# Hybrid decoder trunk on one core: the clearing of the forget gate's tile is moved to the head of GpSimd's row of constants

## The chip, the cores and the metric

The kernel runs on one core of one Trainium2 chip. The metric is the device time of one execution in microseconds. Three executions of the kernel before took 1278.13, 1283.45 and 1277.13 us; their median is 1278.13. A further execution was recorded by the hardware profiler, and all rows below come from that one.

## The reference

Two layers, each with two sub-layers. The first sub-layer is the mixer, which this case is about:

```
u = rms_norm(h, pre_g);  z = u @ w_in
q, k, v, f_logit, a_val, a_gate, sc_b, sc_c, sc_x = split(z)
log_f  = log_sigmoid(f_logit + b_forget)            # 8 heads
y_attn = forgetting_attention(q, k, v, log_f)       # logit[t,s] = q.k/8 + F[t] - F[s], F = cumsum(log_f)
y_conv = silu(layer_norm(conv31(a_val * sigmoid(a_gate)))) @ a_pw_w
y_sc   = sc_b * conv3(sc_c * sc_x)
h     += rms_norm(head_norm([y_attn, y_conv, y_sc]) @ w_out, post_g)
```

The second sub-layer is a gated feed-forward network with a three-tap convolution. The sequence has 512 tokens and 16 learned ones ahead of them, 528 rows in all; the model is 1024 wide.

## The kernel before, in words

Activations lie transposed, features on the 128 partitions and the 528 rows along the free axis, cut into two halves of 264. Each float32 operand is split into a high and a low part (`uhi`, `ulo`; `whi`, `wlo`), and a product takes three TensorE passes (hi*hi, lo*hi, hi*lo). ScalarE casts a landed weight block to its high part (line 608) and VectorE makes the low part (line 612).

The order of the instructions on TensorE, ScalarE, VectorE and GpSimd is written by a planner in the kernel (`Flow`), which carries its own estimates of durations, and it is kept as written: every engine works through its queue strictly in that order. GpSimd's row of constants is not planned. It stands in the source in the order in which it runs.

The mixer of a layer begins with six weight blocks (two for the gate, two for the value of the convolution, then `sc_c` and `sc_x`), whose products are made at line 709. Blocks 1 to 5 lie in the "wide" tiles on the right-hand side of SBUF. When these products have been issued, the pool `ap` is opened over the same memory (line 1025), and its tiles are declared one after the other: `vhi`, `vlo`, `vals`, `causal`, eight `k` tiles, eight `q` tiles, `dm0`, `dm1`, `fx`, `gt`, and smaller ones. GpSimd clears or fills them as they are declared: its row runs from `vhi` (through the helper at line 439) to `causal` (lines 1122 and 1123), four rounds of two pieces of a `k` tile and two of a `q` tile, `dm0` and `dm1`, then `fx` (line 1151), `p4`, `p4w` and last a strip of the tile `both`.

In the compiled program the tiles of `ap` lie in the order in which they are declared, from byte 173,664 of each partition upwards. `fx` has 160 bytes at 228,320. The first `k` tile (`k00`) ends at byte 192,416. The wide tile with the high part of block 5 (`sc_x`) begins at byte 192,480, so `k00` ends 64 bytes short of it. Where a tile of `ap` overlaps a wide tile, its clearing waits for the last product that reads that wide tile: the first `q` tile waits for blocks 2 and 3, the second `k` tile (`k10`) for the last product of block 5. `k00` waits for neither. The layout and these waits are the same in both layers.

Then the projections run on TensorE, in this order near the change: `v` for heads 0 to 3 together with the eight columns of the forget gate, in five blocks of rows b = 0 to 4 (line 1204, and line 1199 for the short block 4, which reads `both`), two halves of `q`, two of `k`, and so on (line 668). The five blocks and the halves after them take PSUM banks 0, 1, 2, 0, 1, 2, ... in turn, so block 3 needs the bank of block 0 back. What empties a block's bank: ScalarE casts the values to `vhi` (line 1180), VectorE adds the bias of the forget gate and writes `fx` (line 1184), then VectorE makes `vlo` (line 1181). Block 4 goes through the copy `vsum` (lines 1218 and 1219).

The forget gate follows: ScalarE's Abs, Exp and Ln (lines 1231 to 1233), VectorE's lines 1234 to 1239 (four running sums into `fpre`, the last of them read by the product at line 1244), the product with a triangle of ones (lines 1243 and 1244), its copy to `gt` (line 1245), and five transposes (line 1253). Between these stand, in VectorE's queue, the taps of the 31-tap convolution (line 937, `cacc`), the taps of the short convolution (lines 987 and 989, `sccx`), low parts of weights and low parts of `q` and `k` (lines 1292 and 1320).

Of the kernel before, what the change touches and what calls it, by code (L numbers as in the profile page):

```python
# [9 lines left out]
F32 = mybir.dt.float32  # L10
# [5 lines left out]
P = 128  # L16
# [6 lines left out]
HEADS = 8  # L23
# [363 lines left out]
def tile_hybrid_trunk(ctx: ExitStack, tc: tile.TileContext, xT, wflat, pv_d, out):  # L387
    nc = tc.nc
# [3 lines left out]
    def T(pool, shape, dt, tag, bufs=None):  # L392
        uid[0] += 1
        kw = {} if bufs is None else {"bufs": bufs}
        return pool.tile(list(shape), dt, tag=tag, name=f"{tag}_{uid[0]}", **kw)
# [498 lines left out]
    def mixer(l, ypool, first, close_first, spans):  # L894
# [130 lines left out]
        ap = ms.enter_context(tc.tile_pool(name=f"ap{l}", bufs=1, side="right", reuse_waits="tile"))  # L1025
# [84 lines left out]
        sc_done = {}  # L1110


        vhi = T(ap, [P, 5, WHOLE, VW], F32R, "vhi")
        vlo = T(ap, [P, 5, WHOLE, VW], F32R, "vlo")
        pw_place[0] = lambda: T(ap, [P, 5, WHOLE, VW], F32R, "vlo").rearrange("p b h d -> p (b h d)")
# [30 lines left out]
        for j in range(2):  # L1146
            dm = T(ap, [P, L], F32R, f"dm{j}")
            mset(dm[:, :N_META], 0.0)
            dms.append(dm)
        fx = T(ap, [P, 5, HEADS], F32, "fx")  # L1150
        nc.gpsimd.memset(fx, 0.0)
        gt = T(ap, [P, 5, HEADS], F32, "gt")
        g_hl = [T(mp, [P, L], F32, "sq", 2)[:HEADS].bitcast(F32R) for _ in range(2)]

# [654 lines left out]
    for l in range(DEPTH):  # L1809
# [15 lines left out]
        with ExitStack() as ms, tc.manual_schedule(engines=every):  # L1825
            flow.yields = YM[l]
            y, y_at, early = mixer(l, ypool, first, wxs.close, i_spans)
# [711 lines left out]
```

## Time and profile before

| | |
|---|---|
| median of three runs | 1278.13 us (1277.13 to 1283.45) |
| the profiled execution | 1277.56 us, of which 1275.8 us span from the first to the last instruction |
| mean granted TensorE clock | 0.995 |
| busy: TensorE, VectorE, ScalarE, GpSimd | 97%, 76%, 61%, 19% of the span |
| TensorE without a product in flight, 50 to 70 us and 70 to 82 us (layer 0) | 0.86 us and 1.38 us |
| the same, 679 to 699 us and 699 to 711 us (layer 1) | 0.65 us and 1.38 us |

A row of a timeline gives the start, the time, the engine, the line, the operation and its tiles; a row that ends in "x2" joins two instructions. What stands in brackets is the idle time of that engine just before, and the instruction that ended it. A row of a list of waits gives who waited for whom, the total in us, how many times, and the longest.

### The profile page before, as it was taken

Reading aid. Unit: us, or ns where it says so; the run is one execution under the profiler, and the core shown is the slowest. Engines: PE = TensorE matmul, PEld = TensorE weight load, DVE = VectorE, ACT = ScalarE, POOL = GpSimd, SP = SyncE. Lnnn points to the kernel's source line nnn. Section 1 sums busy time; section 2 is a strip of 40 time slices with the busy share of each in tenths; the row PEclk is TensorE's granted clock in tenths of the full one; section 3 lists DMA queues with packets and bytes.
Section 4 is the critical chain, followed back from the end, with each engine's and each line's share of the span. In section 5 each row is a group of like instructions: output and inputs, shape, how many; then the busy total and the mean of one; then the engine's idle time right before and its main releaser. Section 6 shows DMA issues by size and latency. Waiting matters only on the chain.

```text
span 1275.8 us, 24511 instructions
## 1 busy us (share of the span) xinstructions
PE 1239.5 (97%) x9468; PEld 1188.3 (93%) x9468; DVE 967.7 (76%) x1752; ACT 775.6 (61%) x1571; POOL 236.2 (19%) x415
## 2 busy tenths in 40 slices
PE   9999999999999999999999999999998999999996
PEld 8988988999999999999999899889997999999986
DVE  7598877588866777788676988766887587778865
ACT  7256668667755555556672666785676565556552
POOL 1314320002122222120003233200022122122200
PEclk9999999999999999999999999999999999999998
DMA  7131131636486866776340322216386677768641
GB/s 225 51 102 52 47 113 34 206 119 167 102 195 139 188 156 154 172 161 183 115 140 18 111 76 68 60 58 213 131 175 136 155 160 169 163 148 185 144 141 66
DMA packets 73942, 165.85 MB, mean 130 GB/s; under 512 B 8081, under 2 KB 26641, under 8 KB 73313
## 3 DMA queue, kind: packets, MB, share of 16 engines
q1 hardware_dynamic: 52048, 124.86, 30.6%
q0 software_dynamic: 21360, 39.02, 19.0%
q8 instruction: 74, 1.21, 0.4%
q10 hardware_dynamic: 416, 0.40, 0.1%
q14 instruction: 44, 0.35, 0.1%
HBM read 129.14 MB, written 8.65 MB: 108 GB/s over the span
## 4 chain that ended last, share of the span: by engine, by line
PE 79%; DVE 8%; ACT 4%; issue 4%; DMA 2%; POOL 2%; DVEq 0%; ACTq 0%; POOLq 0%
PE psum L668 37%; PE psum L2198 25%; PE psum L709 6%; PE psum L1462 2%; PE psum L1204 2%; PE psum L792 2%; PE psum L1405 1%; DVE cacc L937 1%; DMA c<-acc 1%; DMA raw<-in_w_dram 1%; PE psum L1361 1%; POOL q L439 1%; DMA raw<-u 1%; POOL k L439 1%; PE psum L1532 1%
## 5 line engine op out<-in xcount | busy, mean ns | idle before, releaser
L668 PE MATMUL psum<-yhi,whi 128*128 128x264 f32 (+3 forms) x660 | 187.9, 299 | 3.6 <-ACT yp L2373 2.1
L668 PE MATMUL psum<-ylo,whi 128*128 128x264 f32 (+3 forms) x660 | 184.7, 295 | 1.1 <-DVE ylo L2175 0.8
L668 PE MATMUL psum<-yhi,wlo 128*128 128x264 f32 (+3 forms) x660 | 184.3, 294 | 0.2 <-DVE wlo L612 0.2
L668 PE MATMUL psum<-uhi,whi 128*128 128x264 f32 (+1 forms) x640 | 165.2, 291 | 1.2 <-DVE q L1292 1.2
L668 PE MATMUL psum<-ulo,whi 128*128 128x264 f32 (+1 forms) x640 | 161.0, 284 | 0.5 <-DVE ulo L1947 0.5
L668 PE MATMUL psum<-uhi,wlo 128*128 128x264 f32 (+1 forms) x640 | 160.7, 284 | 0.0
L2124 DVE SCALAR_TENSOR_TENSOR c<-z,pv,c 128x528 f32<-128x528 f32 (+1 forms) x156 | 117.1, 757 | 29.0 <-ACT c L2122 26.4
L612 DVE TENSOR_TENSOR wlo<-raw,whi 128x1024 fp32r<-128x1024 f32 (+2 forms) x84 | 100.5, 1205 | 38.1 <-ACT whi L608 37.1
L668 PEld LDWEIGHTS psum<-yhi,whi 128*128 128x128 f32 x660 | 120.3, 188 | 9.1 <-ACT yp L2373 2.5
L668 PEld LDWEIGHTS psum<-ylo,whi 128*128 128x128 f32 x660 | 120.4, 188 | 4.4 <-DVE ylo L1088 1.1
L668 PEld LDWEIGHTS psum<-yhi,wlo 128*128 128x128 f32 x660 | 120.4, 189 | 3.2 <-DVE wlo L612 0.6
L668 PEld LDWEIGHTS psum<-uhi,whi 128*128 128x128 f32 x640 | 111.9, 188 | 4.4 <-issue 2.4
L2211 ACT COPY z<-psum 128x264 f32<-128x264 f32 (+2 forms) x128 | 48.2, 377 | 107.2 <-PE psum L2198 106.5
L668 PEld LDWEIGHTS psum<-ulo,whi 128*128 128x128 f32 x640 | 112.2, 188 | 0.9 <-DVE ulo L1947 0.7
L668 PEld LDWEIGHTS psum<-uhi,wlo 128*128 128x128 f32 x640 | 112.1, 188 | 0.4 <-DVE wlo L612 0.4
L608 ACT CAST whi<-raw 128x1024 fp32r<-128x1024 f32 (+2 forms) x84 | 85.8, 1034 | 38.7 <-DMA raw<-in_w_dram 20.4
L937 DVE SCALAR_TENSOR_TENSOR cacc<-apad,pv,cacc 128x528 f32<-128x528 f32 x120 | 88.6, 766 | 0.3
L709 PE MATMUL psum<-uhi,whi 128*128 128x264 f32 (+1 forms) x320 | 85.0, 289 | 1.3 <-ACT uhi L840 1.3
L709 PE MATMUL psum<-uhi,wlo 128*128 128x264 f32 (+1 forms) x320 | 83.4, 283 | 0.0
L2052 DVE TENSOR_TENSOR wlo<-raw,whi 128x1024 fp32r<-128x1024 f32 (+4 forms) x78 | 76.4, 980 | 8.6 <-ACT whi L2049 8.2
L2049 ACT CAST whi<-raw 128x1024 fp32r<-128x1024 f32 (+4 forms) x78 | 66.3, 855 | 15.5 <-PE psum L668 10.3
L2198 PE MATMUL psum<-uhi,whi 128*128 128x264 f32 (+1 forms) x256 | 72.8, 284 | 2.2 <-ACT yp L2373 2.2
(317 smaller groups left out, 3732.4 us busy)
## 6 DMA issues: line engine op xcount, KB each, us to landing
raw<-in_w_dram SPq DMA_DIRECT2D x110, 512.0 KB
u<-in_w_dram SPq DMA_DIRECT2D x32, 512.0 KB
u<-in_w_dram POOLq DMA_DIRECT2D x32, 256.0 KB, 5.3
raw<-in_w_dram POOLq DMA_DIRECT2D x32, 256.0 KB, 4.1
u<-raw POOLq DMA_DIRECT2D x32, 256.0 KB, 4.0
raw<-u POOLq DMA_DIRECT2D x32, 256.0 KB, 4.2
raw<-in_w_dram SPq DMA_DIRECT2D x16, 448.0 KB
h_mid<-h SPq DMA_DIRECT2D x4, 1056.0 KB
```

The lines of the kernel that those rows point to most:

```text
L439: nc.gpsimd.memset(t.bitcast(F32), val)
L608: nc.scalar.copy(box["hi"][:, :sz], box["raw"][:, :sz])
L612: nc.vector.tensor_sub(lo[:, :sz], box["raw"][:, :sz], box["hi"][:, :sz].bitcast(F32))
L668: nc.tensor.matmul(d, lhsT=w[a][:, k, cols], rhs=rhs(b, k, hf), start=start and i == 0 and p == 0, stop=stop and i == n - 1 and p == 2)
L709: nc.tensor.matmul(self.ps[hf, i], lhsT=self.ws[i].w[a][:, k, :], rhs=self.rhs(b, k, hf), start=k + a + b == 0, stop=k == KD - 1 and b == 1)
L792: nc.tensor.matmul(ps, lhsT=om_d, rhs=box["c"][:, i, :], start=j + i == 0, stop=j + 1 == n_parts and i == 1)
L937: nc.vector.scalar_tensor_tensor(conv[j], in0=src, in1=conv[j], scalar=col("a_dw_w", CK * j + i), op0=ALU.mult, op1=ALU.add)
L2049: nc.scalar.copy(box[name][0], raw())
L2052: return a, dve(dve_us(n), lambda: nc.vector.tensor_sub(box[name][1], raw(), box[name][0].bitcast(F32)), a, prio=prio)
L2124: nc.vector.scalar_tensor_tensor(c, in0=z[:, i:i + n], scalar=wtap(i, t), in1=c, op0=ALU.mult, op1=ALU.add)
L2198: nc.tensor.matmul(d, lhsT=w[i][:, P * k:P * (k + 1)], rhs=terms[b][j][k](), start=start and k + p == 0, stop=k == KH - 1 and p == 2, skip ...
L2211: done[f, name] = act(us, lambda: nc.scalar.copy(z_of(f, e)[:, zin[h]], d[:, lo:]), *after, prio=0)
```

## The change

The tile `fx` is declared, and cleared, at the head of the pool instead of behind `dm1`. Nothing else is touched.

```diff
         sc_done = {}
 
 
+        fx = T(ap, [P, 5, HEADS], F32, "fx")
+        nc.gpsimd.memset(fx, 0.0)
         vhi = T(ap, [P, 5, WHOLE, VW], F32R, "vhi")
...
             mset(dm[:, :N_META], 0.0)
             dms.append(dm)
-        fx = T(ap, [P, 5, HEADS], F32, "fx")
-        nc.gpsimd.memset(fx, 0.0)
         gt = T(ap, [P, 5, HEADS], F32, "gt")
```

Because tiles lie in the order of their declaration, `fx` now has the first 160 bytes of the pool, and every tile from `vhi` to `dm1` lies 160 bytes higher than before. `gt` and the tiles behind it stay where they were.

## The prediction

> **What bounds the kernel now.** I read the page first.
>
> ```profile
> span 1275.8 us, 24511 instructions
> PE 79%; DVE 8%; ACT 4%; issue 4%; DMA 2%; POOL 2%; DVEq 0%; ACTq 0%; POOLq 0%
> ```
>
> TensorE (PE) carries 79% of the chain that ended last, so a gain must take idle time out of TensorE or shorten one of the short detours of that chain through other engines. The edit concerns one tile, so the next view is that of `fx`, and then who waited for whom from 50 to 82 us in layer 0.
>
> ```profile
> L1151 POOL MEMSET fx<- x2: 137/138/138, 60.0 to 689.1; 128x40 f32 x2
> ...
> DVE fx L1184 <- POOL fx L1151: 6.5, 1, 6.5
> ...
> ACT vhi L1180 <- DVE vsum L1219: 2.6, 1, 2.6
> ...
> PE psum L1204 <- DVE vlo L1181: 0.9, 1, 0.9
> ...
> PE psum L1253 <- DVE gt L1245: 0.7, 1, 0.7
> PE psum L1244 <- DVE fpre L1239: 0.7, 1, 0.7
> ```
>
> A clearing of 138 ns holds VectorE (DVE) for 6.5 us, and three waits of TensorE on VectorE stand in the same 32 us. The list for 679 to 711 us of layer 1 has the same three:
>
> ```profile
> PE psum L1253 <- DVE gt L1245: 0.7, 1, 0.7
> PE psum L1244 <- DVE fpre L1239: 0.7, 1, 0.7
> ...
> PE psum L1204 <- DVE vlo L1181: 0.3, 1, 0.3
> ```
>
> They sum to 0.9 + 0.7 + 0.7 = 2.3 us in layer 0 and 1.7 us in layer 1. The question is how many of them follow from the 6.5 us. The timelines of layer 0 say how:
>
> ```profile
> 47.81 0.51 POOL L439 MEMSET vhi<- 128x264 f32 x2
> 53.17 0.49 DVE L987 TENSOR_SCALAR sccx<-cxp,pv 128x528 f32<-128x528 f32 x1
> 54.78 0.37 ACT L1180 CAST vhi<-psum 128x256 fp32r<-128x256 f32 x1 [2.27 <-PE psum L1204]
> 60.04 0.14 POOL L1151 MEMSET fx<- 128x40 f32 x1
> 60.21 0.17 DVE L1184 TENSOR_TENSOR fx<-psum,pv 128x8 f32<-128x8 f32 x1 [6.55 <-POOL fx L1151]
> 60.97 0.42 DVE L1181 TENSOR_TENSOR vlo<-psum,vhi 128x256 fp32r<-128x256 f32 x1
> ```
>
> ScalarE's cast at 54.78 marks when block 0's product was there. VectorE had been free since 53.66 and could have added the bias at 54.8; it did so at 60.21, when GpSimd's row had come to its end. That is 5.4 us late, and all of VectorE's queue stands behind it.
>
> **The change, part by part.**
>
> *The clearing itself.* It moves from the 60.04 place to the head of the row, where `vhi` started at 47.81 right behind the instruction before it. It is one clearing of 138 ns, so `vhi` and what follows slip by at most that much, and `p4`, `p4w` and `both` gain it back. In layer 1 the new place is memory that `vhi` had before, so `fx` takes over the waits that `vhi` had there, which cost no visible time. `fx` is ready at about 48.0 us, 6.8 us ahead of its first use. It has no DMA, and SP's queue is not touched.
>
> *VectorE's queue.* With the bias added at 54.8 the queue runs on: a short-convolution tap, `vlo` of block 0, another tap, two taps of `cacc`, then the next bias. From 60.21 to 60.97 a bias and a tap take 0.76 us, so `vlo` of block 0 begins near 55.6 instead of 60.97, and VectorE waits from then on for blocks 1, 2 and 3 instead of trailing them. TensorE's first stall goes:
>
> ```profile
> 60.17 0.29 PE L1204 MATMUL psum<-whi,ulo 128*128 128x264 f32 x1
> 60.30 0.28 PE L1204 MATMUL psum<-wlo,uhi 128*128 128x264 f32 x1
> 61.44 0.39 PE L1204 MATMUL psum<-whi,uhi 128*128 128x264 f32 x1 [0.86 <-DVE vlo L1181]
> 61.67 0.28 PE L1204 MATMUL psum<-whi,ulo 128*128 128x264 f32 x1
> ```
>
> Products start 0.12 us apart. From 60.30 to 61.67 are two steps, 1.37 us instead of 0.24: the stall is worth 1.13 us, of which 0.86 is shown as idle. Block 3, block 4 and all behind them start 1.1 us earlier.
>
> *The forget gate.* Three rows show how late VectorE was, and two more how TensorE ran into it:
>
> ```profile
> 66.60 0.37 ACT L1218 COPY vsum<-psum 16x264 f32<-16x264 f32 x1 [1.56 <-PE psum L1199]
> 70.00 0.41 DVE L1219 TENSOR_TENSOR vsum<-vsum,psum 16x264 f32<-16x264 f32 x1
> 75.17 0.87 DVE L1292 SCALAR_TENSOR_TENSOR q<-psum,q 64x264 fp32r<-64x264 f32 x2
> 75.67 0.76 ACT L1315 CAST k<-psum 64x264 fp32r<-64x264 f32 x2 [0.35 <-PE psum L668]
> 78.05 0.16 DVE L1239 TENSOR_TENSOR fpre<-fpre,fe 128x8 f32<-128x8 f32 x1
> 77.30 0.31 PE L1243 MATMUL psum<-fe,tri 128*128 128x40 f32 x2
> 78.27 0.41 PE L1244 MATMUL psum<-fpre,ones_r 128*128 128x40 f32 x2 [0.66 <-DVE fpre L1239]
> 79.20 0.28 PE L668 MATMUL psum<-uhi,wlo 128*128 128x264 f32 x1
> 79.93 0.20 DVE L1245 COPY gt<-psum 128x40 f32<-128x40 f32 x1
> 80.19 0.71 PE L1253 MATMUL psum<-ident,gt 128*8 128x128 f32 x5 [0.70 <-DVE gt L1245]
> ```
>
> ScalarE had `vsum` at 66.97 and VectorE took it up at 70.00, 3.0 us late; ScalarE's queue then stood 2.6 us behind that (the wait in the list). After the change `vsum` is there at 65.9 and VectorE is free for it. The last running sum is then bound by TensorE: the second half of `q` ends one half (24 products of 0.122 us, 2.9 us) before the `k` cast at 75.67, at 72.7, and 1.1 us earlier at 71.6. ScalarE's two casts (0.8 us) and VectorE's last part take it to 72.9. From the end of those `q` rows (76.04) to the end of the last running sum (78.21) is 2.2 us, so that sum ends near 75.1. TensorE reaches the pair of line 1243 at 77.30 - 1.13 = 76.2: no wait. Then `gt` needs the product (0.41 us after 76.3, 76.8) and VectorE, which came to it 1.72 us after the last running sum (78.21 to 79.93), now 76.8; with its 0.20 us it ends near 77.0, and TensorE comes to line 1253 after 0.93 + 0.12 us, at 77.4: no wait, by 0.4 us only. Start to start, the two stalls are worth 0.97 - 0.24 = 0.73 and 0.99 - 0.12 = 0.87 us.
>
> *Sum.* By idle time alone 2.2 us in layer 0 and 1.7 in layer 1, 3.9 us; start to start 2.7 and 2.2 us, 4.9 us. (In layer 1 the first stall is shown as 0.3 idle; with 0.27 us of the same slow restart it is 0.57.) I take 4.5 us, nearer to the starts, since these move the later work. The profiled execution's 1277.56 becomes 1273.1; the median shown is 0.6 us above it, so the median after is about 1273.5.
>
> *What becomes late instead.* By the layout, `k00` now reaches 96 bytes into the wide tile of block 5, so its clearing must wait for the last product of line 709.
>
> ```profile
> 50.42 1.13 POOL L439 MEMSET k<- 64x528 f32 x2
> 51.73 0.38 ACT L974 COPY sccx<-psum 128x264 f32<-128x264 f32 x1 [4.22 <-PE psum L709]
> 60.32 0.21 POOL L439 MEMSET both<- 128x128 f32 x1
> 64.47 0.28 PE L1199 MATMUL psum<-whi,both 128*48 128x264 f32 x1
> ```
>
> ScalarE's copy was released by the last product but one, at 51.73; `k00` can start near 51.85 instead of 50.42, 1.4 us later. All the rest of GpSimd's row stands behind it. The one with the earliest user is `both`: it ends near 60.53 + 1.4 = 61.9, and block 4 now wants it at 64.47 - 1.13 = 63.3. So 1.4 us are left, and the new wait costs nothing; in layer 1, where block 4 moves by 0.57 us only, more is left. It would cost, us for us, if the row slipped by over 1.4 us more.
>
> *Beside each other.* After the change VectorE's taps run beside the clearings of 54.8 to 61.9 us, which had SBUF to themselves before. Busy time by stretches (PE, PEld, DVE, ACT, POOL) and one row of the timeline:
>
> ```profile
> 50.40:51.56 1.16, 1.16 (x12) 1.16 (x11) 1.16 (x3) 0.00 (x0) 1.07 (x2) 1.00 0.00 0
> 55.28:56.44 1.16, 1.16 (x12) 1.16 (x11) 0.00 (x0) 0.00 (x0) 1.07 (x2) 1.00 0.00 0
> 52.75 1.39 POOL L439 MEMSET k<- 64x528 f32 x2
> ```
>
> Two clearings took 1.07 us with VectorE busy throughout with taps and 1.07 us with VectorE idle, so taps and clearings don't disturb each other. The pair at 52.75 took 1.39 us beside the TENSOR_SCALAR of 53.17; that one instruction stands beside the row before and after alike. The Trainium skill speaks against the change here: "GPSIMD Engine Reference", section Specifications, has GpSimd contend with VectorE instructions that have two SBUF inputs, which the taps have. By it the change would cost time (the second rival). "SBUF — State Buffer", section Who interferes with whom, restricts that to GpSimd instructions that read SBUF, and a clearing only writes; the 1.07 us on both sides agree with the second page, so the sum stands.
>
> **The rivals.**
>
> *Only the first stall goes.* If ScalarE or the arrival of weights, not VectorE's lateness, sets the forget gate, the waits at lines 1244 and 1253 stay or come back a few products later: the gain is 1.13 + 0.57 = 1.7 us, 1276.5 us. For it: `gt` has 0.4 us of margin in my walk. Against: the 2.6 us that ScalarE itself waited for `vsum`.
>
> *Slower: the row of clearings becomes TensorE's wait.* Were a clearing to be held by each tap beside it, as the 1.39 us pair was held by one instruction, each would wait up to a tap, some 0.7 us (a tap and a bias are 0.76). Four of the 16 large ones take 2.33 us (50.42 to 52.75), so from 51.85 on five are done by 54.8 and 11 are left: 11 * 0.7 = 7.7 us. `both` would end at 61.9 + 7.7 = 69.6, 6.3 us after block 4 wants it, and at worst the same again in layer 1: 12.6 us of stall against 1.7 us of gain, with the forget gate late again, 1288 us. It decides from 1.4 us of slip on. The two 1.07 us stretches speak against it.
>
> *More than the sum.* Layer 0 has further waits of TensorE on the way:
>
> ```profile
> 94.51 0.39 PE L668 MATMUL psum<-uhi,whi 128*128 128x264 f32 x1 [0.61 <-DVE q L1292]
> 115.74 0.39 PE L1385 MATMUL psum<-dm,ones_r 128*128 128x264 f32 x1 [0.65 <-POOL dm L1376]
> ```
>
> If these, too, came from VectorE's backlog, some 1.3 us a layer would be added to the upper sum, 4.9 + 2.6 = 7.5 us, about 1270.5. Against: both stand at the end of chains that start at TensorE, so they move with it.
>
> *No change.* If another release held `fx` at its new place, 1277.5. `vhi` at 47.81 ran at that place without waiting, so this is unlikely.
>
> **How the numbers follow.** The forecast has 0.68, only the first stall 0.12, more than the sum 0.12, slower 0.05, no change 0.03. The range reaches from below the third case to the first: 1269.5 to 1277.0 us; it takes in 3.9 and 4.9 us and leaves out slower, no change and the edges. A measurement of this kernel can tell about 0.5% (6.4 us) from no change; the forecast of 4.5 us is 0.35%, inside that. Faster by over 0.5% (below 1271.7) takes the third case and the forecast's edge, 0.18; slower 0.06; the same 0.76.
>
> **What would show it.** In the profile after: `fx` cleared near 47.9 us; VectorE's first bias near 54.8, with about 1.1 us of idle time before it; no wait of TensorE on `vlo`, `fpre` or `gt`; the vsum add within 0.1 us of ScalarE's copy; line 1253 near 77.4 instead of 80.19, so about 2.7 us earlier, and some 2.2 us more in layer 1; `k00` at 51.85 behind a wait for line 709, and `both` done near 61.9 without TensorE waiting. I am wrong if TensorE waits for `both`, if lines 1244 or 1253 still wait, or if the 4.5 us seen in the mixers are lost again behind them.

## The result, and the profile after

The changed kernel takes 1271.16 us (median of six runs, 1267.65 to 1272.28), the kernel before 1278.02 us (six runs, 1277.13 to 1283.45). The ratio is 0.9942, with a 95% interval of 0.9927 to 0.9957: 0.6% faster. The forecast was 1273.5 us with a range of 1269.5 to 1277.0. The profiled execution took 1272.24 us, against 1277.56 before.

From the page of the changed kernel, the span and the chain that ended last:

```profile
span 1270.5 us, 24515 instructions
PE 80%; DVE 6%; ACT 5%; DMA 5%; issue 3%; POOL 1%; SPq 0%; DVEq 0%; POOLq 0%; ACTq 0%
```

The span is 5.3 us shorter, and VectorE (DVE) and GpSimd (POOL) have gone from 8% and 2% of the chain to 6% and 1%. GpSimd's row and VectorE's queue in layer 0:

```profile
47.68 0.13 POOL L1114 MEMSET fx<- 128x40 f32 x1
51.81 1.13 POOL L439 MEMSET k<- 64x528 f32 x2 [1.51 <-PE psum L709]
61.57 0.20 POOL L439 MEMSET both<- 128x128 f32 x1
53.04 0.76 DVE L987 TENSOR_SCALAR sccx<-cxp,pv 128x528 f32<-128x528 f32 x1
55.13 0.17 DVE L1184 TENSOR_TENSOR fx<-psum,pv 128x8 f32<-128x8 f32 x1 [1.32 <-ACT vhi L1180]
65.75 0.42 DVE L1219 TENSOR_TENSOR vsum<-vsum,psum 16x264 f32<-16x264 f32 x1
74.90 0.16 DVE L1239 TENSOR_TENSOR fpre<-fpre,fe 128x8 f32<-128x8 f32 x1
76.78 0.20 DVE L1245 COPY gt<-psum 128x40 f32<-128x40 f32 x1
```

`fx` is cleared 12.4 us earlier, VectorE's first bias comes at 55.13 instead of 60.21, and its idle time before that is 1.32 us instead of 6.55. Down the queue it is 4.3 us earlier at `vsum` and 3.2 us at the last running sum and at `gt`. The new wait of the first `k` clearing for line 709 is there, 1.51 us long. TensorE (PE) in the same stretch:

```profile
51.53 0.28 PE L1204 MATMUL psum<-whi,uhi 128*128 128x264 f32 x1
60.29 0.29 PE L1204 MATMUL psum<-whi,uhi 128*128 128x264 f32 x1
60.42 0.28 PE L1204 MATMUL psum<-whi,ulo 128*128 128x264 f32 x1
63.21 0.28 PE L1199 MATMUL psum<-whi,both 128*48 128x264 f32 x1
75.72 0.31 PE L1243 MATMUL psum<-fe,tri 128*128 128x40 f32 x2
75.86 0.39 PE L1244 MATMUL psum<-fpre,ones_r 128*128 128x40 f32 x2
77.04 0.71 PE L1253 MATMUL psum<-ident,gt 128*8 128x128 f32 x5
```

No row has a bracket: block 3 follows block 2 without a gap at 60.3, and lines 1244 and 1253 don't wait. One trace of the third stall is left: the list of waits from 50 to 82 us has TensorE's weight loads (PEld) for line 1253 waiting 0.2 us for `gt` (0.9 us before), in layer 1 too.

```profile
PEld psum L1253 <- DVE gt L1245: 0.2, 1, 0.2
```

The good measure of what a mixer gained is the time from block 0's first product to the first transpose of line 1253, since it leaves out shifts from earlier. The rows of before that it needs (the transposes of layer 0, at 80.19, stand in the prediction):

```profile
51.65 0.28 PE L1204 MATMUL psum<-whi,uhi 128*128 128x264 f32 x1
681.19 0.39 PE L1204 MATMUL psum<-whi,uhi 128*128 128x264 f32 x1 [0.35 <-ACT sccx L974]
709.26 0.71 PE L1253 MATMUL psum<-ident,gt 128*8 128x128 f32 x5 [0.70 <-DVE gt L1245]
```

And those of after, layer 1:

```profile
678.58 0.39 PE L1204 MATMUL psum<-whi,uhi 128*128 128x264 f32 x1 [0.35 <-ACT sccx L974]
704.22 0.71 PE L1253 MATMUL psum<-ident,gt 128*8 128x128 f32 x5
```

Layer 0 went from 80.19 - 51.65 = 28.54 us to 25.51, layer 1 from 28.07 to 25.64: 3.0 and 2.4 us, 5.5 us in all. That is the 5.3 us of the span, to 0.2 us.

### The profile page after: what moved, and what is told of

The parts are those of the page before. It is cut to its first block, busy times and chain, and to the rows that moved or that the text cites. A ratio compares the mean times of both kernels' runs of the same rounds, so it can differ in the third digit from the quotient of the medians.

```text
span 1270.5 us, 24515 instructions
## 1 busy us (share of the span) xinstructions
PE 1237.3 (97%) x9468; PEld 1187.7 (93%) x9468; DVE 969.2 (76%) x1752; ACT 775.3 (61%) x1571; POOL 236.4 (19%) x415
## 4 chain that ended last, share of the span: by engine, by line
PE 80%; DVE 6%; ACT 5%; DMA 5%; issue 3%; POOL 1%; SPq 0%; DVEq 0%; POOLq 0%; ACTq 0%
PE psum L668 37%; PE psum L2198 25%; PE psum L709 6%; PE psum L1204 4%; DMA raw<-in_w_dram 3%; PE psum L1462 2%; PE psum L1405 1%; PE psum L792 1%; DMA c<-acc 1%; PE psum L1361 1%; DVE wlo L612 1%; PE psum L1199 1%; DMA raw<-u 1%; POOL pf L1423 1%; ACT whi L608 1%
```

## The experiments

Theory A: `fx` came late, VectorE's whole queue stood behind it, and TensorE ran into that lateness three times a mixer; only the time of the clearing counts. The rivals: the shift of the tiles by 160 bytes does something (C), or the cost grows evenly with the lateness (D). The first four kernels ran on one chip with a median of 1276.10 us for the kernel before (15 runs); the last four ran on another and shared 26 runs of it (1276.42 us). An edit can move the line numbers in the rows by one or two: L1203 after the third round is L1204 before. The diffs for the old layout leave out the lines that declare the tiles in the old order and the ones that drop the clearing at its old place, where these are not shown.

**The changed kernel once more.**

> The changed kernel once more, as the measure for the others on this chip. Its six runs spread from 1267.65 to 1272.28 us, its profiled span was 5.3 us shorter than before, its median 6.9 us. Theory A (the gain is TensorE's three stalls a mixer, which VectorE's late start caused): the profile shows no wait of TensorE on vlo, fpre or gt again, line 1253 near 77.0 us, and a time about 5 to 7 us below the kernel before. Theory B (part of the gain is chance of these runs): 3 to 4 us below.

Measured: 1269.77 us, ratio 0.9948 (0.9936 to 0.9961), 6.3 us less by medians. None of the three waits, and 25.52 and 25.65 us for the two stretches. Theory A as to the mechanism. The medians again differ by more than the 5.5 us of the stretches, but the interval (5.0 to 8.2 us) holds those 5.5, and theory B's 3 to 4 us lie outside it.

**Early, in the old layout.** All tiles are declared first, in the old order; only then does the row begin, with `fx`.

> fx is cleared at the head of the row, but all tiles are declared in the old order, so they lie where they lay before. Theory A (only the time of the clearing counts): k00 is cleared at about 50.5 us again without waiting for line 709, both ends near 60.5 instead of 61.8, and the time is that of the changed kernel within 1 us. Rival C (the shift of the tiles by 160 bytes gives or takes something): over 1.5 us away from the changed kernel.

```diff
         vals = T(ap, [P, 5, WHOLE, VW], F32, "vals")
+        ...                                         # causal, kh, qh and dms, declared here in the old order
+        fx = T(ap, [P, 5, HEADS], F32, "fx")
+        nc.gpsimd.memset(fx, 0.0)
         for t, one in ((vhi, 1.0), (vlo, 0.0), (vals, 1.0)):
...
-        fx = T(ap, [P, 5, HEADS], F32, "fx")
-        nc.gpsimd.memset(fx, 0.0)
```

Measured: 1269.78 us, ratio 0.9948 (0.9935 to 0.9962): the same as the changed kernel. GpSimd's row no longer waits:

```profile
50.28 1.12 POOL L439 MEMSET k<- 64x528 f32 x2
60.05 0.20 POOL L439 MEMSET both<- 128x128 f32 x1
```

The 1.5 us by which the changed kernel delays the rest of the row cost nothing, and the layout gives nothing.

**The layout alone.** `fx` is declared first and cleared at its old place. The diff is against the changed kernel.

> fx is declared first, so all tiles lie as in the changed kernel, but it is cleared at its old place in the row. Theory A: the row is 1.3 us late because k00 waits for line 709, so fx comes near 61.3 us instead of 60.0, VectorE waits some 7.5 us for it, and TensorE's stall at block 3 grows by as much in layer 0 (0.86 to about 2.2 us) and layer 1; the other two stalls stay as they were, since they follow at the same distance. Sum 2.5 us slower than before, 1280.5 us. Rival C (the layout is what gains): faster than before.

```diff
         fx = T(ap, [P, 5, HEADS], F32, "fx")
-        nc.gpsimd.memset(fx, 0.0)
...
             dms.append(dm)
+        nc.gpsimd.memset(fx, 0.0)
```

Measured: 1279.71 us, ratio 1.0024 (1.0013 to 1.0035), about 3 us slower than before. In layer 0:

```profile
61.54 0.17 DVE L1184 TENSOR_TENSOR fx<-psum,pv 128x8 f32<-128x8 f32 x1 [7.72 <-POOL fx L1151]
62.77 0.39 PE L1204 MATMUL psum<-whi,uhi 128*128 128x264 f32 x1 [2.30 <-DVE vlo L1181]
```

The stall at block 3 went from 0.86 to 2.30 us, in layer 1 from 0.3 to 1.7; those at lines 1244 and 1253 stayed at 0.7. So the shift by itself harms, through the longer wait for `fx`, and rival C falls. It also shows that the change is two things: with `fx` still cleared near the end of the row, the same shift is a loss.

**Early in layer 0 only**, in the old layout.

> Old layout; fx is cleared early in layer 0 only, at its old place in layer 1. Theory A: layer 0 as in the changed kernel (line 1253 3.1 us earlier than before), layer 1 with the three waits of before (0.3, 0.7, 0.7 us); in all 2.5 to 3.5 us faster than before, 1275 us. If the gain of one layer depended on the other, or were lost in between, the time would lie outside 1273.5 to 1276.

```diff
+        if l == 0:
+            nc.gpsimd.memset(fx, 0.0)               # head of the row
...
+        if l == 1:
+            nc.gpsimd.memset(fx, 0.0)               # old place
```

Measured: 1273.11 us, ratio 0.9976 (0.9965 to 0.9987), 3.0 us less than before. The stretches are 25.51 us in layer 0 and 28.09 us in layer 1, those of the changed kernel and of before. The time lies below the 1273.5 us that the expectation had as its lower limit; that limit goes with the 1278.02 us that the kernel before took in the first comparison, and it took 1276.10 us here. As a difference the 3.0 us are inside the expected 2.5 to 3.5. The layers add up, and what layer 0 gains is not lost behind it.

**After the third round, and before the last one's `q`.** Both in the old layout; `fx` is cleared inside the row.

> Old layout; fx is cleared after the third of the four rounds of k and q clearings, near 57.4 us, so VectorE's first bias comes about 6.1 us after block 0's first product in layer 0 and 5.7 us in layer 1 (3.6 and 3.7 in the changed kernel, 8.6 and 8.1 before). Theory A with a margin: VectorE can make up for lateness until the bias comes 5.6 us after that product, because it has idle time further on; beyond that each microsecond costs TensorE one. From block 0's first product to line 1253: about 26.0 us in layer 0 and 25.8 in layer 1 (25.5 and 25.6 changed, 28.5 and 28.1 before); about 4.7 us faster than before. Rival D (the cost grows evenly with the lateness from the start): 27.0 and 26.7 us, about 2.8 us faster than before.

```diff
             mset(qh[i][0][aux + 32:aux + 64], 0.0)
+            if i == 2:
+                nc.gpsimd.memset(fx, 0.0)
```

> Old layout; fx is cleared between the k and the q of the last round, near 58.5 us: the bias comes about 7.3 us after block 0's first product in layer 0, 6.9 us in layer 1. Theory A with a margin: 1.7 us and 1.3 us over the margin, so 27.2 us and 26.9 us from that product to line 1253, 2.4 us faster than before. Rival D: 27.7 and 27.3, 1.6 us faster than before. All of the time should stand as waits on fpre and gt (lines 1244 and 1253), with a first wait on vlo at block 3 only if vlo ends later than 60.4 us.

```diff
             mset(kh[i][0][mrow], 1.0)
+            if i == 3:
+                nc.gpsimd.memset(fx, 0.0)
```

Measured: 1270.53 us, ratio 0.9951 (0.9933 to 0.9969), and 1274.92 us, ratio 0.9991 (0.9978 to 1.0004). By the intervals the first is 4.0 to 8.6 us faster than before, which leaves out rival D's 2.8 us; the second lies between 2.8 us faster and 0.5 us slower, which leaves out neither. The rows separate the two sharply. After the third round:

```profile
51.27 0.28 PE L1203 MATMUL psum<-whi,uhi 128*128 128x264 f32 x1
57.42 0.17 DVE L1183 TENSOR_TENSOR fx<-psum,pv 128x8 f32<-128x8 f32 x1 [4.14 <-POOL fx L1148]
77.39 0.71 PE L1252 MATMUL psum<-ident,gt 128*8 128x128 f32 x5 [0.57 <-DVE gt L1244]
```

and before the last `q`:

```profile
51.26 0.28 PE L1203 MATMUL psum<-whi,uhi 128*128 128x264 f32 x1
58.56 0.17 DVE L1183 TENSOR_TENSOR fx<-psum,pv 128x8 f32<-128x8 f32 x1 [5.30 <-POOL fx L1146]
76.61 0.41 PE L1243 MATMUL psum<-fpre,ones_r 128*128 128x40 f32 x2 [0.66 <-DVE fpre L1238]
78.53 0.70 PE L1252 MATMUL psum<-ident,gt 128*8 128x128 f32 x5 [0.69 <-DVE gt L1244]
```

Counted from block 0's first product, in us:

| kernel | bias, layer 0 | transposes, layer 0 | bias, layer 1 | transposes, layer 1 |
|---|---|---|---|---|
| changed | 3.60 | 25.51 | 3.68 | 25.64 |
| after the third round | 6.15 | 26.12 | 5.69 | 25.67 |
| before the last `q` | 7.30 | 27.27 | 6.86 | 26.84 |
| before | 8.56 | 28.54 | 8.10 | 28.07 |
| layout alone | 10.00 | 29.98 | 9.51 | 29.48 |

In every row but the first the transposes come 19.97 to 19.98 us after the bias: VectorE's queue between the two has no slack left and sets TensorE's time, microsecond for microsecond. In the first row they come 21.9 us after it, because VectorE has to wait in between (brackets of 0.38, 0.15, 0.36 and 0.63 us in its rows of layer 0) for ScalarE, whose casts follow TensorE's products: there TensorE sets the time. The bend lies at 25.5 - 20.0 = 5.5 us after block 0's first product, 1.9 us behind the place where the bias comes now. Before, the bias came 8.56 - 3.60 = 5.0 us later than now: 1.9 us of that were taken up by idle time further down VectorE's queue (1.5 us of it are those four brackets), and 3.0 us reached TensorE. That lateness up to the bend costs nothing is best seen in layer 1, where the bias comes 2.0 us later after the third round than in the changed kernel and the transposes 0.03 us. VectorE's wait after the third round is still 4.14 us, two thirds of that before, and costs 0.6 us: rival D (27.0 us there) falls.

**A later end of the row.** Five more clearings ahead of `both` in the changed kernel; they write columns that are overwritten later. The diff is against the changed kernel.

> The changed kernel with five more clearings of a 528-column tile ahead of the clearing of both (2.8 us of extra work for GpSimd, whose results are overwritten later). The prediction has it that GpSimd's row costs nothing until both ends 1.4 us later in layer 0, and then costs TensorE us for us. both would end near 64.5 us, 1.3 us after block 4 wants it (63.2) in layer 0, and 0.8 us after it in layer 1: TensorE waits for POOL at line 1199, and the time is about 2 us slower than the changed kernel. If the forget gate, which then has more time, takes up part of it, 1 us or less; if the row were already at its limit, 5 us.

```diff
         both = T(mp, [P, KD, VB], F32R, "both")
+        for _ in range(5):
+            mset(dms[0][:, :], 0.0)
         mset(both[:, :, N_META:32], 0.0)
```

Measured: 1273.02 us, ratio 0.9969 (0.9957 to 0.9982). The clearings took 2.9 us, and TensorE waits:

```profile
64.68 0.20 POOL L439 MEMSET both<- 128x128 f32 x1
64.93 0.32 PE L1201 MATMUL psum<-whi,both 128*48 128x264 f32 x1 [1.32 <-POOL both L439]
```

1.3 us in layer 0 and 0.7 us in layer 1. The stretches to the transposes are 27.03 and 26.57 us, 1.5 and 0.9 us longer: 2.4 us, where about 2 were expected. The changed kernel did not run on this chip; the next kernel, which has the changed kernel's stretches, took 1270.72 us on it, 2.3 us less. So the row had 1.4 us to spare, as the prediction put it, and the forget gate takes up none of it.

**Cleared once.** One tile of 160 bytes for both layers, cleared with the constants at the program's start. The diff is against the changed kernel.

> fx is one tile for both layers, cleared once with the constants at the start of the program; no clearing of fx in the mixers. In the second layer the rows that no bias is written to hold the zeros that the first layer left. Theory A: VectorE finds it ready as in the changed kernel, so the time is that of the changed kernel within 1 us, 5 to 7 us faster than before. The clearing itself (0.13 us on GpSimd) was never what cost.

```diff
     c_one = const_col("c_one", 1.0)
+    fx = T(const, [P, 5, HEADS], F32, "fx")
+    nc.gpsimd.memset(fx, 0.0)
...
-        fx = T(ap, [P, 5, HEADS], F32, "fx")
-        nc.gpsimd.memset(fx, 0.0)
```

Measured: 1270.72 us, ratio 0.9958 (0.9946 to 0.9970), with stretches of 25.50 and 25.64 us: the changed kernel's time, with one clearing less. No kernel of these beats the changed one beyond its interval.

## Why the prediction was right, and where not

*The mechanism held.* A clearing of 0.13 us cost TensorE 5.5 us, because it stood near the end of a row that took 12 us, and everything in VectorE's queue stood behind its reader. All three waits of TensorE went, none came in their place, and what gains is the time of the clearing, not the layout.

*The first bias at 54.8.* It came at 55.13. I had overlooked that the bias comes behind ScalarE's cast of the same PSUM bank, which the row's bracket names: the cast of 54.65 ends at 55.03, 0.10 us before the bias. In layer 1 the row names a clearing of `k` as what ended the wait. It is the same cast there: that cast ends 0.09 us before the bias, and in the kernel that clears `fx` once the same row of layer 1 names the cast, at the same distance from block 0's first product (3.63 us, 3.68 in the changed kernel). The 0.3 us cost nothing, being within the 1.9 us of slack.

*The forget gate without waits.* Right for VectorE: 75.06 for the end of the last running sum (75.1 predicted), 76.78 for the start of `gt`'s copy (76.8). The 0.4 us of margin at line 1253 were not there. TensorE reached line 1243 at 75.72, not 76.2, so it came to line 1253 earlier than in my walk, and its weight load waited 0.2 us for `gt`. The transposes began at 77.04, 0.25 us after the product before them, where 0.12 is the usual step: 0.13 us of the third stall are left.

*The new wait of `k00`.* Right: it starts at 51.81 (51.85), `both` ends at 61.77 (61.9), block 4 wants it at 63.21 (63.3), and the kernel with a later end of the row shows the price, microsecond for microsecond beyond 1.4.

*Taps beside clearings.* Right. Two clearings that VectorE's taps accompany throughout take 1.08 us in the changed kernel, as the row of stretches shows (PE, PEld, DVE, ACT, POOL):

```profile
56.60:57.76 1.16, 1.16 (x12) 1.16 (x11) 1.16 (x3) 0.19 (x1) 1.08 (x2) 1.00 0.00 0
```

So the slower rival had nothing to stand on. Of the two pages of the Trainium skill that the prediction sets against each other, these 1.08 us agree with "SBUF — State Buffer", section Who interferes with whom, by which a VectorE instruction with two SBUF inputs doesn't contend with a GpSimd instruction that only writes SBUF.

*The sum was too small.* "I take 4.5 us" is the term that was off: the stretches gained 3.0 + 2.4 = 5.5 us. Adding up idle times (3.9 us) misses the slow restart behind each stall, and even the sum from start to start (4.9 us) lacked a fourth stall, a wait of the weight loads for VectorE's `wlo`, which stood behind the same lateness. The list of waits has it, and the products before and after it:

```profile
PEld psum L668 <- DVE wlo L612: 0.2, 1, 0.2
...
72.39 0.28 PE L668 MATMUL psum<-ulo,whi 128*128 128x264 f32 x1
72.69 0.39 PE L668 MATMUL psum<-uhi,wlo 128*128 128x264 f32 x1
72.92 0.29 PE L668 MATMUL psum<-uhi,whi 128*128 128x264 f32 x1
```

Matching TensorE's products of before and after one by one gives what each stall was worth, in us:

| stall | layer 0, predicted | layer 0, measured | layer 1, predicted | layer 1, measured |
|---|---|---|---|---|
| block 3 (`vlo`) | 1.13 | 1.13 | 0.57 | 0.56 |
| weight load (`wlo`) | 0 | 0.28 | 0 | 0.28 |
| line 1244 (`fpre`) | 0.73 | 0.85 | 0.73 | 0.85 |
| line 1253 (`gt`) | 0.87 | 0.74 | 0.87 | 0.73 |

The errors at lines 1244 and 1253 cancel, so the missing 0.5 us are the weight load, 0.28 us in each layer. The table of distances further up gives the shorter rule: not the sum of the stalls, but how far the reader's queue was late where TensorE met it last, 8.56 us against 5.54 at the bend, and 8.10 against 5.67.

*The medians moved further than the stretches*, by 6.9 and 6.3 us, and "faster by over 0.5%", to which I gave 0.18, is what came out, by a little. The interval of the first comparison (5.5 to 9.3 us) begins where the stretches end. I found no second mechanism in the traces; that the medians moved by more than the stretches is not shown to come from the change, and whether something adds up to 1 us outside the mixers stays open, since the runs scatter by more than that (below).

*More than the sum.* The waits at 94.51 and 115.74 are still there after, 0.61 and 0.65 us, at the end of chains that begin at TensorE: that rival falls.

## What to carry to other kernels

Where small constants are cleared in the order of their declaration, sort them by first use: the cost of a late clearing is not its own time but the lateness that it puts on the whole queue of its reader. To price such a wait, find how much idle time the reader's queue has further down before the bottleneck engine meets it; only what is left beyond that counts, and from there on each microsecond counts in full. And a moved tile moves its neighbours: check which of them now overlap memory that somebody still reads, and how much time that row has.

## What the runs showed of the hardware that was not expected

*TensorE's clock falls to half for 3.4 us in some executions, behind idle times of 1.4 to 2.1 us.* The column PEclk of the stretches (the first number behind the five engines) shows it, here for the kernel before, where TensorE had stood idle for 2.09 us up to 983.50, and below for the kernel that clears `fx` once and for the changed one, at the same place of the program:

```profile
980.00:985.00 5.00, 2.91 (x11) 2.02 (x10) 3.06 (x5) 1.73 (x3) 0.84 (x1) 0.86 0.88 213
985.00:990.00 5.00, 5.00 (x25) 4.52 (x24) 0.69 (x1) 0.89 (x2) 0.86 (x1) 0.80 0.98 249
```

```profile
1220.00:1225.00 5.00, 2.81 (x20) 2.28 (x19) 3.14 (x5) 2.47 (x4) 0.00 (x0) 1.00 1.01 381
1225.00:1230.00 5.00, 5.00 (x45) 5.00 (x44) 2.52 (x3) 4.17 (x8) 0.00 (x0) 1.00 0.04 14
```

```profile
1220.00:1225.00 5.00, 3.07 (x22) 2.67 (x20) 2.39 (x4) 1.68 (x3) 0.00 (x0) 0.93 1.05 375
1225.00:1230.00 5.00, 5.00 (x33) 5.00 (x33) 2.44 (x3) 5.00 (x9) 0.00 (x0) 0.73 0.14 55
```

In the kernel before, 0.14 + 0.20 of two stretches of 5 us are missing, 1.7 us of full clock; single microseconds inside them show 0.50, so the half clock lasted 3.4 us. Two idle times of 1.3 and 0.8 us left the clock alone in one execution, and 1.1 and 0.8 us brought it down in another, where 33 products ran in 5 us instead of 45: some 1.4 us lost. Apart from the program's start and its last 15 us, the profiled executions had such stretches in different numbers and places, the kernel before one and the changed kernel one, so they cancel in the 5.3 us; the layout alone had two, one of them at 80 us, behind the stalls of the forget gate (0.66 and 0.70 us), where it lost another 1.5 us. The same two stalls left the clock at 1.00 in the kernel before; why such idle times bring it down in one execution and not in another, no run here shows.

The lower clock is a good part of why equal kernels scatter by 2 to 7 us: of the 26 runs of the kernel before, the three with the lowest mean granted clock (0.991 to 0.993) average 1280.0 us and the four with the highest (0.997) 1274.7 us. It is not all: between the two mixers, from line 1253 of layer 0 to block 0 of layer 1, the nine traces with no such stretch there differ by 2.1 us (601.0 to 603.1).

*A TENSOR_SCALAR and the clearings beside it get in each other's way.* The prediction had this instruction stand beside the row alike before and after. The one at 53.04 took 0.76 us in the changed kernel, and its counterpart 0.49 us before. In both cases a pair of clearings beside it is longer, too: the pair of `q` clearings at 52.98 took 1.30 us after, the pair of `k` clearings at 52.75 took 1.39 us before, against 1.10 and 1.13 elsewhere in the row. VectorE was idle right behind it in both kernels, so it cost nothing here. The taps, which have two inputs in SBUF, show nothing of the kind.
